# Operands of the products moved to multiples of 512 bytes from the weights, and the first block's 1/rms applied on VectorE alone

## Chip, cores and metric

The kernel runs on one core of one Trainium2 chip. The metric is device time in microseconds, the median of several executions. One more execution was profiled; its trace is what the rows below are read from.

## What is computed

Two blocks follow one another on a sequence of 2048 positions with 1024 features, in float32. The first norms x, multiplies it with w_in, and splits the result into a state space mixer (s5, with a gelu and a gated w_glu product) and a short convolution; both meet in w_out, a residual and a second norm. The second block has a modulation from w_ada, a convolution of seven taps, a two-way scan in chunks of 128 (ssd), a Fourier mix, an output product w_out2 and a gated feed-forward layer of width 2816.

```python
xn = rmsnorm(h, norm_gain[l])
proj = jnp.einsum('bld,dc->blc', xn, w_in[l])
...
v = gate_c * h                          # short_conv_mixer
y = sum(conv_w[k] * vp[:, k:k + seq] for k in range(CONV_K))
return gate_b * y
...
(jax.nn.silu(h @ w_gate) * (h @ w_up)) @ w_down      # swiglu
```

In the first block h, gate_c, gate_b and z_conv are all columns of proj, so each carries the factor 1/rms of its position.

## The kernel before

Features lie on the 128 partitions, positions along the free axis. The sequence is cut into four blocks of TB = 512 positions, and every large product works on one block: an output tile of 128 features by 512 positions is the sum over KD = 8 (or fewer) slices k of 128 input features.

Each float32 product is done as three products of a rounded type. `weights` (L100 to L112) loads a row of weights, wraw, of 4096 bytes per partition (issued by the SP queue, L106), rounds it into whi on ScalarE (L108) and takes the rest into wlo on VectorE (L111). The data is split the same way into a high and a low tile, such as xh and xl. `gemm` then issues 2 matmuls for each k with whi (L122 with the high, L123 with the low tile) and, after these, one for each k with wlo (L126). Every matmul has a weight load (PEld) of its own, of 128 columns or 512 bytes per partition; the moving operand is 512 columns or 2048 bytes. Slices of weights step by 512 bytes, slices of the data by 2048, so the distance between the two, modulo 512 bytes, is one and the same for all matmuls of a kind.

Which products have which data:

- xh, xl (L122, L123, L126): all of the first block's products and the second block's w_in2 and w_out2. The first norm's data for ctx has 256 columns.
- yh, yl: the four w_glu tiles of each block, four slices each.
- dxh, dxl: w_gate and w_up of the feed-forward layer, 44 tiles for each block of positions.
- hh, hl: w_down, in parts of three to five slices. The last part of the last block is done in two halves of 256 columns, with weights of its own in a pool e.
- uf (L1146 to L1148): here a slice of xh or xl is the stationary operand and 280 columns of a constant pair wfh, wfl move. A slice of those steps by 1120 bytes.

Where the tiles lie follows from the pools, which are stacked in the order in which they are opened: const, w, norm and hx (xh, xl) from the low end of a partition, others from the high end. After the feed-forward layer's start, hx is closed and the pool d with hh and hl begins where hx began. Every tile takes a multiple of 32 bytes. The norm pool holds 18 tiles of 16 bytes, which take 576 bytes, 64 more than 512; all else in w and norm is a multiple of 512. The addresses in a partition, in bytes, and their distance from the weights:

```
tile        first address            distance from whi and wlo, modulo 512
whi, wlo    32416 and 40608          -
xh, xl      67808 (and 3 more)       64
hh, hl      67808 (and 9 more)       64
dxh, dxl    176832, 193216           32
yh, yl      212960, 221152           320
```

In the last block's halves, hh and its weights in pool e are at distance 0. In uf the moving wfh is at distance 0 from xh at k = 0, and each k adds 1120 bytes; wfl is 256 further.

The order of the instructions of each engine is the program's, with priorities where `high_priority` raises them; each engine and each DMA queue works through its own list in order.

In block 0 the norm isn't applied to x ahead of the products: `first_prep` puts x times the gain into xh, xl, and 1/rms, as the tile r0 (128x512), is multiplied into the results. `h(j)` (L799) makes hs from a product: VectorE multiplies it by r0 (L803) and POOL by r0 again (L804), since hs meets a second unscaled product in `c(j)` (L815, cv). After the three taps POOL multiplies the sum cy by r0 (L825), and `g(j)` (L830) multiplies the next product into it. POOL also builds the s5 tables T at the time (L404 to L409, six products a step, from `s5_params`); a table is stored by a DMA of the SP queue (L620, Td). Next to these, `a1_prep` norms the next block's x: n_t on VectorE (L741), then xh on ScalarE and xl on VectorE (L137, L138).

`rstd` (L153) computes 1/rms from a sum of squares in some twelve tiny instructions on tiles of 128x4, in two buffers each; rs_b is one of them.

Of the kernel before, what the change touches and what calls it, by code (L numbers as in the profile page):

```python
# [10 lines left out]
F32R = mybir.dt.float32r  # L11
I32 = mybir.dt.int32
AF = mybir.ActivationFunctionType
ALU = mybir.AluOpType
# [3 lines left out]
P = 128  # L18
D = 1024
KD = 8  # L20
SEQ = 2048
TB = 512
# [39 lines left out]
class Kernel:  # L62
    def __init__(self, ctx, tc, A, stage=99):
        self.ctx, self.tc, self.A, self.nc = ctx, tc, A, tc.nc
        self.stage = stage
        self.uid = 0
        self.pool_lo = False
        self.ahead = 75


    def nm(self, s):
        self.uid += 1
        return f"{s}_{self.uid}"
# [79 lines left out]
    def rstd(self, acc, width, y=None):  # L153


        nc = self.nc
        c = acc.shape[1] // P
        ps = self.bank("nb", (P, c))
        for i in range(c):
            nc.tensor.matmul(ps[:, i:i + 1], lhsT=acc[:, i * P:(i + 1) * P],  # L160
                             rhs=self.ones[:, 0:1], start=True, stop=True)

        def tl(s, dt=F32):
            return self.t(self.np_, (P, c), f"rs_{s}", dt, bufs=2)

        v, h, y0, y1 = tl("v"), tl("h", I32), tl("y0"), tl("y1")
        y = self.t(self.np_, (P, c), "rs_y", bufs=6) if y is None else y
        nc.vector.tensor_scalar(v, ps, 1.0 / width, EPS, ALU.mult, ALU.add)
        nc.vector.tensor_single_scalar(h, v.bitcast(I32), 1, ALU.arith_shift_right)
        nc.vector.tensor_scalar(y0.bitcast(I32), h, -1.0, 1597463007.0, ALU.mult, ALU.add)  # L170
        a, b = tl("a"), tl("b")
        nc.vector.tensor_tensor(a, y0, y0, ALU.mult)
        nc.vector.tensor_tensor(a, a, v, ALU.mult)
        nc.vector.tensor_scalar(b, a, 0.375, -1.25, ALU.mult, ALU.add)
        nc.vector.tensor_tensor(b, b, a, ALU.mult)
        nc.vector.scalar_tensor_tensor(y1, b, 1.875, y0, ALU.add, ALU.mult)
        nc.vector.tensor_tensor(a, y1, y1, ALU.mult)
        nc.vector.tensor_tensor(a, a, v, ALU.mult)
        nc.vector.tensor_scalar(a, a, -0.5, 1.5, ALU.mult, ALU.add)
        nc.vector.tensor_tensor(y, y1, a, ALU.mult)  # L180
        return y
# [212 lines left out]
    def s5_params(self, pp):  # L394

        nc, A = self.nc, self.A
        st = {}

        def tl(s, sh=(P, NG), bufs=1):
            return self.t(pp, sh, s, bufs=bufs)  # L400
# [10 lines left out]
        def first():  # L411
# [74 lines left out]
            a, b = tl("pa", (P, NG, 8)), tl("pb", (P, NG, 8))  # L486
            for m in (1, 2, 4, 8):
                yield
                n = min(m, 15 - m)
# [14 lines left out]
            yield  # L504
            nc.vector.tensor_copy(self.E128[:, 0], Hr[:, :, 8])
            nc.vector.tensor_copy(self.E128[:, 1], Hi[:, :, 8])
            zero = tl("zero", (P, 1024))
            nc.vector.memset(zero, 0.0)
            for q in range(4):
                nc.sync.dma_start(out=self.Md[:, 8 * q:8 * q + 8, :],  # L510
                                  in_=zero.rearrange("p (g c) -> p g c", c=P))
            st["dsk"] = tl("dsk", (GH, NG))
            nc.sync.dma_start(out=st["dsk"], in_=A["s5_d"])
# [104 lines left out]
        def store(bt):  # L618

            nc.sync.dma_start(out=self.Td[bt], in_=st["T"])  # L620

        units = self.steps(first, 15)
        for bt in range(NG // G):
            units += self.steps(lambda bt=bt: matrices(bt), 3)
# [148 lines left out]
    def a1_units(self, b, ops):  # L773
        nc, A = self.nc, self.A
        st = {}
        tb, hf = divmod(b, 2)

        def mt(m):
            return self.mtile(A["w_in"][m], ops[b])

        def silu(out, ps):
            if b == 0:
                nc.vector.tensor_tensor(out, ps, self.r0, ALU.mult)
                ps = out
            nc.scalar.activation(out, ps, AF.Silu)

        def u(j):
            ps = mt(j)
            us = self.tmp("us")
            kt = lambda v: v.rearrange("p (k t) -> p k t", t=T8)  # L790
            uk = us.rearrange("p (t k) -> p k t", t=T8)
            if b == 0:
                nc.vector.tensor_tensor(uk, kt(ps), kt(self.r0), ALU.mult)
            else:
                nc.scalar.copy(uk, kt(ps))
            nc.sync.dma_start(out=self.Ud[tb, j * P:(j + 1) * P, :, hf * 64:(hf + 1) * 64],
                              in_=us.rearrange("p (t k) -> p t k", t=T8))

        def h(j):  # L799
            ps = mt(8 + j)  # L800
            st["hs"] = self.tmp("hs")
            if b == 0:
                nc.vector.tensor_tensor(st["hs"], ps, self.r0, ALU.mult)  # L803
                nc.gpsimd.tensor_tensor(st["hs"], st["hs"], self.r0, ALU.mult)  # L804
            else:
                nc.scalar.copy(st["hs"], ps)

        def c(j):
            ps = mt(16 + j)
            v = self.tmp("cv", (P, TB + 2))  # L810
            if b == 0:
                nc.vector.memset(v[:, 0:2], 0.0)
            else:
                nc.vector.tensor_copy(v[:, 0:2], self.ccarry[:, j])
            nc.vector.tensor_tensor(v[:, 2:], ps, st["hs"], ALU.mult)  # L815
            if b + 1 < NB:
                nc.vector.tensor_copy(self.ccarry[:, j], v[:, TB:TB + 2])
            y = self.tmp("cy")
            nc.vector.tensor_scalar(y, v[:, 2:], self.vec("conv_w", 8 + j), None, ALU.mult)
            nc.vector.scalar_tensor_tensor(y, v[:, 1:TB + 1], self.vec("conv_w", 4 + j), y,  # L820
                                           ALU.mult, ALU.add)
            nc.vector.scalar_tensor_tensor(y, v[:, 0:TB], self.vec("conv_w", j), y,
                                           ALU.mult, ALU.add)
            if b == 0:
                nc.gpsimd.tensor_tensor(y, y, self.r0, ALU.mult)  # L825
            st["y"] = y

        def g(j):
            ps = mt(12 + j)
            nc.vector.tensor_tensor(st["y"], ps, st["y"], ALU.mult)  # L830

        def z(j):
            ps = mt(20 + j)
            zs = self.tmp("zs")
            silu(zs, ps)
            nc.vector.tensor_tensor(zs, st["y"], zs, ALU.mult)
            nc.sync.dma_start(out=self.YCd[b, :, j], in_=zs)

        def zs(j):
            ps = mt(4 + j)  # L840
            t = self.tmp("zs")
            silu(t, ps)
            nc.sync.dma_start(out=self.ZSd[b, :, j], in_=t)

        units = [lambda j=j: u(j) for j in range(4)]
        for j in range(4):
            units += [lambda j=j, f=f: f(j) for f in (h, c, g, z)]
        units += [lambda j=j: zs(j) for j in range(4)]
        return units
# [860 lines left out]
    def run(self):  # L1710
# [3 lines left out]
        with ExitStack() as eh:  # L1714
            self.hp = self.pool("hx", 2, ctx=eh)
            left = self.run_ab(ops)
            if left is None:
                return
            self.ahead = 40
            g3, ((g1, prep1), (g2, prep2)) = left  # L1720
            self.tp = self.pool("tmpc", ctx=eh)
            with ExitStack() as es:
                u = self.ssd_units(3, self.pool("c", ctx=es))
                W(u[:4], g3[:3])
                W(u[4:10])
                W(u[10:13], g3[3:])
                W(u[13:28], prep2)
                W(u[28:], g2[:4])
            xp = self.pool("dx", side="right")

            def room():
                return tuple(self.t(xp, (P, KD, TB), n, F32R) for n in ("dxh", "dxl"))

            def dprep(b):
                return self.mod_prep(lambda k: self.X2d[b, :, k], lambda: self.rs[b],
                                     self.s2_x, self.sf_x, TB, ops, ("d", b), room)

            prep, prod, res = self.mix_units(3, self.hx, self.pool("o3", ctx=eh))
            W(prep, g2[4:])
            W(prod, prep1)  # L1740
            W(res + dprep(3), g1)
# [4 lines left out]
        for b in range(NB - 1, -1, -1):  # L1746
            main, cost, tail, res, ending = self.ffn_units(b, ops, dp)
            n = FQ[1]
# [20 lines left out]
    def run_ab(self, ops):  # L1769
# [4 lines left out]
        with ExitStack() as es:  # L1774
# [3 lines left out]
            with self.tc.high_priority(offset=30):  # L1778
                self.first_prep(ops)
            with ExitStack() as e2:  # L1780
                params = self.s5_params(self.pool("s5p", ctx=e2))
                n = len(params) // 2
                W(self.a1_units(0, ops), self.merge(params[:n], self.a1_prep(1, ops)))
                W(self.a1_units(1, ops), self.merge(params[n:], self.a1_prep(2, ops)))
# [19 lines left out]
        with ExitStack() as es:  # L1804
# [10 lines left out]
            n = (0, 9, 18, 27, 34)  # L1815
# [132 lines left out]
```

## Time and profile before

| | us |
|---|---|
| median of 3 runs (lowest, highest) | 3682.25 (3679.05, 3688.32) |
| the profiled execution | 3681.94 |
| its span, first to last instruction | 3680.1 |
| PE busy | 3507.8 |
| VectorE (DVE) busy | 2145.9 |
| ScalarE (ACT) busy | 1459.8 |
| GpSimd (POOL) busy | 988.2 |

The span leaves out 1.8 us of the execution's time. PE is TensorE's matmuls, PEld its weight loads, SPq the queue that issues most DMAs. The mean granted clock of TensorE is 0.98 of full speed. Matmul durations are modelled and overlap one another, so the pace of a run of matmuls is read from starts, not from durations.

### The profile page before, as it was taken

The numbers are of one execution on the slowest core, as the hardware profiler recorded it, in microseconds if no ns is written. First come the engines' busy times: TensorE is split into PE (matmuls) and PEld (weight loads), VectorE is DVE, ScalarE is ACT, GpSimd is POOL, SyncE is SP. The second block draws the span as 40 slices with busy tenths as digits, with TensorE's granted clock in tenths as the row PEclk, the third lists the DMA queues.
The fourth block names the chain that finished last, engine by engine and source line by source line (L and its number), as shares of the span: only waits on it lengthen the run. The fifth ranks groups of instructions, "written<-read, shape, count | busy, mean of one in ns | idle before, by whom it ended". The sixth has DMA issues, their size and how long they took to land. (4 is left out here: it accounts for less than half of the span.)

```text
span 3680.1 us, 46968 instructions
## 1 busy us (share of the span) xinstructions
PE 3507.8 (95%) x16602; PEld 2828.3 (77%) x16602; DVE 2145.9 (58%) x3986; ACT 1459.8 (40%) x2350; POOL 988.2 (27%) x938
## 2 busy tenths in 40 slices
PE   8799999898979999999999999999999999999998
PEld 6577888776778888776777788877888778887787
DVE  8764534456686677777666535665445664454334
ACT  3233232234444344335536533355333553333222
POOL 2864233232453353433223101131011210110001
PEclk9999999999989999999999999999999999999999
DMA  6457665677654565466554335443344433344232
GB/s 197 153 180 215 201 204 177 190 224 246 214 188 162 172 202 174 165 199 196 166 187 138 111 109 166 149 139 115 109 144 158 141 120 110 125 150 133 78 110 77
DMA packets 321932, 588.14 MB, mean 160 GB/s; under 512 B 73888, under 2 KB 150560, under 8 KB 320800
## 3 DMA queue, kind: packets, MB, share of 16 engines
q1 hardware_dynamic: 321696, 585.13, 50.2%
q8 instruction: 132, 2.16, 0.2%
q14 instruction: 104, 0.85, 0.1%
HBM read 472.63 MB, written 112.36 MB: 159 GB/s over the span
## 5 line engine op out<-in xcount | busy, mean ns | idle before, releaser
L108 ACT CAST whi<-wraw 128x1024 fp32r<-128x1024 f32 (+3 forms) x634 | 567.9, 897 | 1058.4 <-PE mm L123 772.1
L111 DVE TENSOR_TENSOR wlo<-wraw,whi 128x1024 fp32r<-128x1024 f32 (+3 forms) x516 | 539.8, 1047 | 725.5 <-PE mm L126 502.5
L122 PE MATMUL mm<-xh,whi 128*128 128x512 f32 (+1 forms) x2000 | 806.2, 405 | 64.9 <-ACT whi L108 42.5
L123 PE MATMUL mm<-xl,whi 128*128 128x512 f32 (+1 forms) x2000 | 790.7, 397 | 3.6 <-DVE xl L138 1.6
L148 POOL TENSOR_TENSOR n_acc<-n_acc,n_sq 128x512 f32<-128x512 f32 (+1 forms) x175 | 229.8, 1317 | 1371.7 <-ACT n_sq L147 1344.1
L123 PE MATMUL mm<-dxl,whi 128*128 128x512 f32 x1408 | 557.6, 396 | 0.8 <-DVE dxl L995 0.6
L122 PE MATMUL mm<-dxh,whi 128*128 128x512 f32 x1408 | 555.8, 395 | 1.9 <-ACT dxh L994 1.9
L122 PEld LDWEIGHTS mm<-xh,whi 128*128 128x128 f32 x2000 | 387.0, 194 | 156.7 <-ACT whi L108 53.4
L126 PE MATMUL mm<-xh,wlo 128*128 128x512 f32 (+1 forms) x2000 | 498.6, 391 | 4.8 <-DVE wlo L111 4.8
L123 PEld LDWEIGHTS mm<-xl,whi 128*128 128x128 f32 x2000 | 386.6, 193 | 86.2 <-DVE xl L138 4.4
L126 PEld LDWEIGHTS mm<-xh,wlo 128*128 128x128 f32 x2000 | 372.5, 190 | 86.5 <-DVE wlo L111 8.0
L111 POOL TENSOR_TENSOR wlo<-wraw,whi 128x1024 fp32r<-128x1024 f32 (+1 forms) x118 | 284.8, 2416 | 558.9 <-ACT whi L108 269.2
L126 PE MATMUL mm<-dxh,wlo 128*128 128x512 f32 x1408 | 360.5, 397 | 0.0
L123 PEld LDWEIGHTS mm<-dxl,whi 128*128 128x128 f32 x1408 | 264.0, 188 | 65.6 <-DVE dxl L995 2.0
L122 PEld LDWEIGHTS mm<-dxh,whi 128*128 128x128 f32 x1408 | 263.7, 187 | 64.4 <-ACT dxh L994 3.2
L126 PEld LDWEIGHTS mm<-dxh,wlo 128*128 128x128 f32 x1408 | 264.1, 188 | 63.8
L122 PE MATMUL mm<-hh,whi 128*128 128x512 f32 (+1 forms) x744 | 285.8, 391 | 2.5 <-ACT hh L137 2.3
L1035 DVE SCALAR_TENSOR_TENSOR cy<-mm,vecs,cy 128x504 f32<-128x504 f32 (+5 forms) x396 | 266.5, 689 | 30.4 <-ACT cy L1029 27.3
L123 PE MATMUL mm<-hl,whi 128*128 128x512 f32 (+1 forms) x744 | 280.7, 383 | 1.4 <-DVE hl L138 1.3
L126 PE MATMUL mm<-hh,wlo 128*128 128x512 f32 (+1 forms) x744 | 195.9, 380 | 0.0
L122 PEld LDWEIGHTS mm<-hh,whi 128*128 128x128 f32 x744 | 139.5, 188 | 33.0 <-ACT hh L137 5.6
L123 PEld LDWEIGHTS mm<-hl,whi 128*128 128x128 f32 x744 | 140.2, 188 | 30.2 <-DVE hl L138 5.0
(472 smaller groups left out, 4547.2 us busy)
## 6 DMA issues: line engine op xcount, KB each, us to landing
wraw<-w_in SPq DMA_DIRECT2D x186, 512.0 KB, 4.5
wraw<-w_gate SPq DMA_DIRECT2D x88, 512.0 KB, 3.6
wraw<-w_up SPq DMA_DIRECT2D x88, 512.0 KB, 3.5
wraw<-w_out SPq DMA_DIRECT2D x64, 512.0 KB, 3.8
mraw<-w_ada SPq DMA_DIRECT2D x96, 256.0 KB, 3.6
n_x<-xT SPq DMA_DIRECT2D x85, 256.0 KB, 4.7
n_x<-X1d SPq DMA_DIRECT2D x80, 256.0 KB, 4.1
n_x<-X2d SPq DMA_DIRECT2D x72, 256.0 KB, 3.8
```

The lines of the kernel that those rows point to most:

```text
L108: nc.scalar.copy(hi, raw)
L111: eng.tensor_tensor(lo, raw, hi.bitcast(F32), ALU.subtract)
L122: nc.tensor.matmul(ps, lhsT=hi[:, s], rhs=xh, start=k == ks[0], stop=False)
L123: nc.tensor.matmul(ps, lhsT=hi[:, s], rhs=xl, start=False, stop=False)
L126: nc.tensor.matmul(ps, lhsT=lo[:, s], rhs=rhs(k)[0], start=False, stop=k == ks[-1])
L148: nc.gpsimd.tensor_tensor(acc, acc, sq, ALU.add)
L1035: nc.vector.scalar_tensor_tensor(yr[:, :, lo:hi], pr[:, :, lo + d:hi + d], w(k), yr[:, :, lo:hi], ALU.mult, ALU.add)
```

## The change

Three edits move tiles. `rstd` takes its rs_b tiles (two buffers of 32 bytes) from the const pool, which lies ahead of the weights, and no longer from norm, which lies behind them: whi and wlo go up by 64 bytes, to 32480 and 40672, and hx and all behind it stay. A tile of 120 columns (480 bytes), written once by POOL, is allocated behind dxh and dxl, which move from 176832 to 176352. Between weights and xh, hh and dxh the distance is then a multiple of 512; yh and yl are at 256.

In block 0, hs is made by one VectorE multiplication with r02 = r0 x r0, a new tile that VectorE computes once, and VectorE does the multiplication of cy. To make room for r02, the tile of zeros that clears Md in DRAM is halved and stored eight times, not four.

```diff
+    def shift(self, pool, n):
+        self.nc.gpsimd.memset(self.t(pool, (P, n), "shift"), 0.0)
...
-        a, b = tl("a"), tl("b")
+        a, b = tl("a"), self.t(self.cp, (P, c), "rs_b", bufs=2)
...
-            zero = tl("zero", (P, 1024))
+            zero = tl("zero", (P, 512))
             nc.vector.memset(zero, 0.0)
-            for q in range(4):
-                nc.sync.dma_start(out=self.Md[:, 8 * q:8 * q + 8, :],
+            for q in range(8):
+                nc.sync.dma_start(out=self.Md[:, 4 * q:4 * q + 4, :],
                                   in_=zero.rearrange("p (g c) -> p g c", c=P))
...
             if b == 0:
-                nc.vector.tensor_tensor(st["hs"], ps, self.r0, ALU.mult)
-                nc.gpsimd.tensor_tensor(st["hs"], st["hs"], self.r0, ALU.mult)
+                nc.vector.tensor_tensor(st["hs"], ps, self.r02, ALU.mult)
...
             if b == 0:
-                nc.gpsimd.tensor_tensor(y, y, self.r0, ALU.mult)
+                nc.vector.tensor_tensor(y, y, self.r0, ALU.mult)
...
             def room():
-                return tuple(self.t(xp, (P, KD, TB), n, F32R) for n in ("dxh", "dxl"))
+                x = tuple(self.t(xp, (P, KD, TB), n, F32R) for n in ("dxh", "dxl"))
+                if not self.shifted:
+                    self.shifted = True
+                    self.shift(xp, 120)
+                return x
...
-                params = self.s5_params(self.pool("s5p", ctx=e2))
+                pp = self.pool("s5p", ctx=e2)
+                self.r02 = self.t(pp, (P, TB), "r02")
+                self.nc.vector.tensor_tensor(self.r02, self.r0, self.r0, ALU.mult)
+                params = self.s5_params(pp)
```

## Rows read from the trace of the kernel before

**Rows 1.** The page: head and part 1, busy time by engine (cut).

```profile
span 3680.1 us, 46968 instructions
PE 3507.8 (95%) x16602; PEld 2828.3 (77%) x16602; DVE 2145.9 (58%) x3986; ACT 1459.8 (40%) x2350; POOL 988.2 (27%) x938
```

**Rows 2.** Windows by stage: length; busy us (count) of PE, PEld, DVE, ACT, POOL; clock; DMA.

```profile
15.00:60.00 45.00, 41.86 (x186) 33.21 (x186) 43.62 (x189) 14.54 (x20) 13.58 (x9) 1.00 0.68 206
...
120.00:180.00 60.00, 43.58 (x175) 33.62 (x176) 46.62 (x75) 17.91 (x29) 49.56 (x78) 0.86 0.59 185
...
1866.00:3667.00 1801.00, 1778.16 (x8048) 1415.33 (x8048) 930.04 (x1567) 729.68 (x1211) 243.68 (x239) 1.00 0.41 127
```

**Rows 3.** PE's groups by line and form; count, busy us, mean ns, idle before.

```profile
L122 PE MATMUL mm<-xh,whi 128*128 128x512 f32 x1920 | 782.7, 409 | 59.3 <-ACT whi L108 42.5 <-ACT xh L758 7.5 <-ACT xh L137 6.4
...
L122 PE MATMUL mm<-dxh,whi 128*128 128x512 f32 x1408 | 555.8, 395 | 1.9 <-ACT dxh L994 1.9
...
L122 PE MATMUL mm<-hh,whi 128*128 128x512 f32 x664 | 266.0, 403 | 2.5 <-ACT hh L137 2.3
```

**Rows 4.** Windows of unbroken products, PE alone: length, busy (count), clock, DMA.

```profile
3578.75:3634.75 56.00, 56.00 (x242) 1.00 0.36 113
1793.49:1836.08 42.59, 42.59 (x187) 1.00 0.52 163
3266.67:3289.57 22.90, 22.90 (x101) 1.00 0.69 207
892.03:900.05 8.02, 8.02 (x36) 1.00 0.69 229
1061.34:1064.16 2.82, 2.82 (x26) 1.00 0.12 47
3636.57:3650.95 14.38, 14.38 (x121) 1.00 0.01 2
1379.35:1391.58 12.23, 12.23 (x97) 1.00 0.57 190
```

**Rows 5.** Timeline of PE, 112 to 129 us: start, length, what, idle before.

```profile
112.95 2.00 PE L126 MATMUL mm<-xh,wlo 128*128 128x512 f32 x8
...
125.77 0.80 PE L122 MATMUL mm<-xh,whi 128*128 128x512 f32 x1 [9.41 <-ACT whi L108]
126.36 0.63 PE L123 MATMUL mm<-xl,whi 128*128 128x512 f32 x1
...
128.92 0.63 PE L123 MATMUL mm<-xl,whi 128*128 128x512 f32 x1
```

**Rows 6.** Timeline of DVE, 105 to 133 us.

```profile
105.26 0.67 DVE L803 TENSOR_TENSOR hs<-mm,r 128x512 f32<-128x512 f32 x1
...
121.51 0.69 DVE L815 TENSOR_TENSOR cv<-mm,hs 128x512 f32<-128x512 f32 x1 [9.81 <-POOL hs L804]
...
131.97 0.69 DVE L830 TENSOR_TENSOR cy<-mm,cy 128x512 f32<-128x512 f32 x1 [3.29 <-POOL cy L825]
```

**Rows 7.** Timeline of POOL, 105 to 121 us.

```profile
105.74 2.26 POOL L407 TENSOR_TENSOR a<-Hr,Li 128x128 f32<-128x128 f32 x1
...
114.35 0.40 POOL L405 TENSOR_TENSOR a<-Hi,Li 128x128 f32<-128x128 f32 x1
...
120.22 1.26 POOL L804 TENSOR_TENSOR hs<-hs,r 128x512 f32<-128x512 f32 x1
```

**Rows 8.** Timeline of the SP queue, 119 to 121 us.

```profile
119.45 0.34 SPq L620 DMA_DIRECT2D Td<-T  x1
119.88 0.38 SPq L106 DMA_DIRECT2D wraw<-w_in  x1
```

**Rows 9.** Timeline of ACT at 123 us.

```profile
122.89 0.62 ACT L137 CAST xh<-n_t 128x512 fp32r<-128x512 f32 x1 [20.58 <-DVE n_t L741]
```

**Rows 10.** POOL's groups, first 200 us.

```profile
L804 POOL TENSOR_TENSOR hs<-hs,r 128x512 f32<-128x512 f32 x4 | 11.0, 2745 | 13.7 <-DVE hs L803 13.7
...
L825 POOL TENSOR_TENSOR cy<-cy,r 128x512 f32<-128x512 f32 x4 | 6.9, 1714 | 16.9 <-DVE cy L822 16.9
```

More of the change, by code (lines that the diff above doesn't have):

```diff
@@ L66, in __init__ @@
         self.uid = 0
-        self.pool_lo = False
+        self.pool_lo = self.shifted = False
         self.ahead = 75
+    def shift(self, pool, n):
+        self.nc.gpsimd.memset(self.t(pool, (P, n), "shift"), 0.0)
     def nm(self, s):
```

## The prediction

> **What bounds the kernel now.** I read the page's head first, then windows by stage, PE's groups, windows of PE alone inside unbroken products, and last the timelines of the first block. PE is busy for 95% of the span [rows 1]. In the feed-forward stretch, 1866 to 3667 us, it is busy for 1778 of 1801 us [rows 2]: nothing else can set the time there, and only a shorter matmul shortens it. One early stretch differs: from 120 to 180 us PE works 43.6 of 60 us and the mean granted clock is 0.86 [rows 2].
>
> So the question is what one matmul costs. The durations in PE's groups, 395 to 409 ns [rows 3], overlap one another and don't answer it. Inside a stretch without a break, the length divided by the starts in it does. A window's count holds, beside those, one or two instructions that began before it, so I divide by 240, 186, 100, 35, 24, 120 and 95 for the seven windows [rows 4]:
>
> - dxh and dxl, 512 columns: 56.00/240 = 233.3 ns
> - xh and xl: 42.59/186 = 229.0 ns
> - hh and hl: 22.90/100 = 229.0 ns
> - yh and yl: 8.02/35 = 229.1 ns
> - ctx, 256 columns: 2.82/24 = 117.5 ns
> - the last block's down products, 256 columns: 14.38/120 = 119.8 ns
> - uf, 280 columns: 12.23/95 = 128.7 ns
>
> All at full granted clock, so load of the DMA and the clock don't divide them: the slowest of the 512 column kinds has a DMA share of 0.36, the quick ones 0.52 to 0.69. What divides them in the same order is where the moving operand lies, modulo 512 bytes, from the weights: 32 for dxh, 64 for xh and hh, 320 for yh, 64 for ctx, 0 for the last block.
>
> How much is there to be had? At half the granted clock the same xh matmul has six starts in 128.92 - 126.36 = 2.56 us [rows 5], 426.7 ns, which is 512 columns at 1.2 GHz with nothing over. At 2.4 GHz the like would be 213.3 ns. So a full-speed matmul loses 15.7 ns at distance 64 and 20.0 ns at distance 32, and loses nothing at half speed. Something that is hidden at half speed collides at full speed, and it depends on the address. The weight load that runs beside each matmul is the one other stream of that kind.
>
> **The change part by part.** *dxh and dxl, distance 32 to 0.* The weights move up by the 64 bytes of two rs_b buffers, dxh down by 480, so the distance becomes 32 - 480 - 64 = -512. Three groups of 1408 [rows 3] are 4224 matmuls. No row has 512 columns at distance 0. Bounds: from below the 213.3 ns of [rows 5], a gain of 4224 x 20.0 = 84 us; from above the present 233.3, no gain. I take 229.0, because the two multiples of 64 that are on show, 64 and 320, give the same time [rows 4] and 0 is the next one: 4224 x 4.3 = 18.2 us gained. The stretch is PE's, so all of it shows.
>
> *xh, xl, hh, hl, distance 64 to 0.* Three groups of 1920 and of 664 [rows 3] are 7752 matmuls. Bounds: 213.3 ns, a gain of 122 us, and 233.3 ns as the worst distance on show, a loss of 33 us. I take no change, again because 64 and 320 agree. One pair of rows says otherwise: at 256 columns distance 0 costs 119.8 ns and distance 64 costs 117.5 ns [rows 4]. There the matmul is half as long while the weight load beside it is the same 128 columns, so I don't carry the 2.3 ns over, but it stands in the range. The 240 ctx matmuls go from 64 to 0: 0.6 us lost by that pair. yh and yl, 192 matmuls, end at distance 256, not 0: a multiple of 64 still, no change.
>
> The Trainium skill, "TensorE: Matmul & The Clock Gate", section "Step-by-step: what each phase is for", says that loading the next tile's weights takes no SBUF read bandwidth from the running matmul; the 229.0 against 233.3 ns of this trace does not agree with a loss of nothing. The same page's section "Back-to-back issue gap" gives N/2.4 + 2.5 ns for a warm matmul, 215.8 ns at 512 columns; as an estimate from that figure, alignment to it would be worth 176 us, about 3500 us in all.
>
> *The first block's factors on VectorE.* Removed from POOL: four hs products and four cy products, 17.9 us of POOL time [rows 10]. Added to DVE: four cy products and one r0 x r0, each like the 0.67 to 0.69 us of DVE's own 512-column products [rows 6], 3.4 us; the hs product on DVE stays, with another factor. What the removal frees is seen at 105 us. DVE wrote hs by 105.93, POOL came to it at 120.22 behind the s5 tables in its queue [rows 7], and DVE stood 9.81 us before cv [rows 6]. Behind cv on DVE are the n_t products, behind them ACT's xh, idle for 20.58 us [rows 9], behind that the cast of the next weights, and PE stands 9.41 us [rows 5]. The c product ends at 112.95 + 2.00 = 114.95, so cv could start 6.5 us sooner, and the next product too.
>
> Where does it go? The SP queue holds a table store, Td, until POOL has written the table, at 119.45, and the next weight load, wraw, is behind it at 119.88 [rows 8]. It stays late, and the product after next waits for it. POOL gets slower when DVE works: its 0.40 us product while DVE stood [rows 7] took 2.26 us at 105.74. So the lasting gain is POOL's saved time on this chain: two hs and two cy, 4 x 1.3 = 5 us by the 1.26 us that an undisturbed one takes, and some of the cold clock. I take 6 us. Bounds: 15 us if the waits of 9.81 and 3.29 us [rows 6] both go and nothing replaces them; 3 us lost if DVE's 3.4 us land in 15 to 60 us, where it is busy 43.62 of 45 us [rows 2].
>
> *The rest.* Eight stores of half a zero tile for four are four more issues on SP, some 0.4 us each by [rows 8], 1.5 us past which one weight load might be moved; the halved memset gives DVE back about as much as r0 x r0 takes. One POOL memset of 120 columns, when POOL is 14% busy [rows 2], is hidden. I count these as nothing, and 1.5 us if the cover is gone.
>
> **Sum.** The profiled execution took 3681.9 us, 1.8 us around its span, and is 0.3 us under the median of the runs shown, so the forecast serves both. 3681.9 - 18.2 - 6 + 0.6 = 3658 us.
>
> **The rivals.** *Clear run.* If the moving stream reads at twice the pace of the weight load, at distance 0 it starts with it and meets it again, 512 bytes on, just as the load ends: few collisions would be left. For it: the loss vanishes at half clock, so it is a matter of meeting. Against it: in uf the moving operand's distance goes through all eight multiples of 32 modulo 256 (the step is 1120 bytes a k), and the mean still has 128.7 - 116.7 = 12.0 ns over 280 columns at 2.4 GHz; one quick case in eight could hide there, but the last block at 0 is not quick. At 5 ns under 229.0: 7752 x 5 + 4224 x 9.3 = 78 us, with the 6 about 3598 us.
>
> *Aligned is worse.* The 256-column pair is right, and both streams asking for the same place at each start costs 2.3 ns more at 512 columns as well: 7752 x 2.3 - 4224 x 2.0 - 6 = +3, 3685 us, no change. If distance 0 costs what 32 does, 233.3 ns: +33 - 6, 3709 us, slower. It decides against the change from 2.9 ns upward: 11976 x 2.9 = 35 against 18.2 + 6 + 11.
>
> *Addresses do nothing.* The 4.3 ns go with dxh for another reason (its place at the far end of the partition, say), and the change doesn't do what it says. By the Trainium skill's rule on weight loads above, this is the case to expect. Only the first block is left: 3676 us, no measurable change. Against it: yh lies at the far end too and takes 229.1 ns [rows 4].
>
> **How the numbers follow.** A difference under 0.3%, 11 us, can't be told from no change here. Chances: dxh as quick as xh 0.43 (3658; its own range 3645 to 3671, the first block's bounds); clear run 0.24; addresses do nothing 0.12; aligned worse 0.21, half of it within 11 us of before and half beyond. Faster: 0.43 + 0.24, with a little of the third case, 0.68. Same: 0.20. Slower: 0.12. The range reaches to 3595, which takes in the clear run to 5 ns, and to 3690, which takes in aligned-worse to 3 us short of the point where it shows, 3693.
>
> **What would show it.** The same seven windows in the changed kernel: dxh at 229 ns is my forecast, 224 or less the clear run, 231 and more for xh the aligned-worse case, 233.3 and 229.0 unchanged the third. uf and the last block must stay at 128.7 and 119.8 ns, since neither distance changes. In the first block the 9.41 us gap before 125.77 should be mostly gone and a wait for wraw, behind Td, stand in its place; DVE should wait for POOL nowhere between L803 and L830. I am wrong in the main if xh moves by more than 2 ns either way, as 7752 matmuls carry each ns as 8 us.

## The result, and the profile after

The changed kernel takes 3640.92 us (median of 4 runs, 3638.66 to 3645.58), the kernel before beside it 3680.65 us (4 runs, 3676.82 to 3688.32): ratio 0.989, 95% interval 0.987 to 0.991. It is faster, by 40 us, where 24 were forecast. The profiled execution took 3638.66 us.

The head and the busy times of the changed kernel's page, then its windows by stage (columns as in [rows 2]):

```profile
span 3636.9 us, 46981 instructions
...
PE 3472.3 (95%) x16602; PEld 2831.2 (78%) x16602; DVE 2146.6 (59%) x3991; ACT 1461.8 (40%) x2350; POOL 968.9 (27%) x931
```

```profile
15.00:60.00 45.00, 41.81 (x189) 33.45 (x188) 43.59 (x191) 14.47 (x20) 12.09 (x8) 1.00 0.71 212
...
120.00:180.00 60.00, 42.85 (x170) 32.92 (x169) 40.53 (x71) 17.49 (x28) 51.24 (x81) 0.91 0.60 190
1866.00:3627.00 1761.00, 1734.92 (x7988) 1404.71 (x7988) 919.52 (x1555) 724.88 (x1204) 243.50 (x238) 1.00 0.41 128
```

The last of these is 40 us shorter than the 1801 us of [rows 2]; it holds 60 matmuls fewer, some 14 us at 229 ns each, and the rest is gain. PE is still what bounds it. Of the 43 us between the two profiled executions, the starts of PE's matmuls give 18 to what lies before the first dxh (1878.8 us before, 1860.7 after) and 25 to the feed-forward stretch behind it. The 18 are two single executions and rough: `e3_dx_alone` below issues the same matmuls as before up to its first dxh and gets there at 1866.3 us.

The windows that the prediction named, PE alone, in the order of [rows 4] (dxh, xh, hh, yh, ctx, the last block, uf); the steps in them, from one start to the next, are 240, 186, 100, 34, 22, 120 and 94:

```profile
2241.16:2295.56 54.40, 54.40 (x241) 1.00 0.69 225
1775.17:1817.36 42.19, 42.19 (x187) 1.00 0.50 164
2301.94:2324.63 22.69, 22.69 (x101) 1.00 0.65 206
875.89:883.65 7.76, 7.76 (x36) 1.00 0.69 231
1010.25:1012.89 2.64, 2.64 (x25) 1.00 0.58 217
3593.17:3607.56 14.39, 14.39 (x121) 1.00 0.01 2
1233.81:1245.92 12.11, 12.11 (x95) 1.00 0.45 142
```

| operand (distance before, after) | before, ns | forecast | after, ns |
|---|---|---|---|
| dxh (32, 0) | 233.3 | 229.0 | 226.7 |
| xh (64, 0) | 229.0 | 229.0 | 226.8 |
| hh (64, 0) | 229.0 | 229.0 | 226.9 |
| yh (320, 256) | 229.1 | 229.1 | 228.2, most steps 226 to 227 |
| ctx, 256 columns (64, 0) | 117.5 | 119.8 | 120.0 |
| last block, 256 columns (0, 0) | 119.8 | 119.8 | 119.9 |
| uf (all, all) | 128.7 | 128.7 | 128.8 |

The two that don't move stayed. The 512-column kinds came to one pace, one that no row of before shows (yh's window has some slower steps in it). In the trace before, the steps went 226, 229, 232 and again (xh), or 231, 235, 233, 234 (dxh); after, nearly every step in these windows is 226 or 227.

In the first block, PE's product that waited 9.41 us in [rows 5], and gaps of PE between 120 and 180 us (idle before, and what ended it):

```profile
115.35 1.05 PE L584 MATMUL ss<-C,X 128*16 128x128 f32 x8
116.33 0.50 PE L126 MATMUL mm<-xh,whi 128*128 128x512 f32 x1
...
123.25 0.50 PE L126 MATMUL mm<-xh,whi 128*128 128x512 f32 x1 [1.19 <-ACT whi L112]
...
131.10 3.67 PE L130 MATMUL mm<-xh,wlo 128*128 128x512 f32 x8 [3.93 <-DVE wlo L115]
...
164.56 0.50 PE L126 MATMUL mm<-xh,whi 128*128 128x512 f32 x1 [2.59 <-ACT whi L112]
...
178.23 0.79 PE L126 MATMUL mm<-xh,whi 128*128 128x512 f32 x1 [6.32 <-ACT whi L112]
```

The wait of 9.41 us of [rows 5] is gone: that product now starts at 116.33 for 125.77 us, without a gap. The product behind it waits 1.19 us, where it waited 1.72. No wait of DVE for POOL is left in the first 200 us. But the time is partly given back. The 16th weight cast whi (casts are counted from 0) comes 15.3 us sooner than before (109.4 for 124.7 us), the 20th 7.5 (148.1 for 155.6), the 24th 6.5 (183.2 for 189.8). Two views of the changed kernel show what took it. The SP queue:

```profile
117.08 0.34 SPq L624 DMA_DIRECT2D Td<-T  x1
117.51 0.38 SPq L110 DMA_DIRECT2D wraw<-w_in  x1
...
135.04 0.33 SPq L624 DMA_DIRECT2D Td<-T  x1
135.46 0.38 SPq L110 DMA_DIRECT2D wraw<-w_in  x1
```

ACT, 139 to 175 us:

```profile
139.99 1.04 ACT L112 CAST whi<-wraw 128x1024 fp32r<-128x1024 f32 x1 [3.99 <-DMA wraw<-w_in]
...
174.61 0.63 ACT L151 ACTIVATE n_sq<-n_x 128x512 f32<-128x512 f32 x1 [10.10 <-POOL n_acc L152]
```

The table store Td still holds the weight load wraw, as in [rows 8]. And the 6.32 us of PE at 178 us have another cause: the weight cast on ACT stands behind a square, n_sq, that waits for POOL's sum n_acc. The sum comes at 173.32 us, behind the tables in POOL's queue:

```profile
172.96 0.40 POOL L409 TENSOR_TENSOR a<-Hi,Li 128x128 f32<-128x128 f32 x1
173.32 3.95 POOL L152 TENSOR_TENSOR n_acc<-n_acc,n_sq 128x512 f32<-128x512 f32 x3
```

The same hold is in the trace before, where ACT waits three times for n_acc in the first 260 us, 11.2 us in all, the longest just ahead of a weight cast:

```profile
184.85 0.63 ACT L147 ACTIVATE n_sq<-n_x 128x512 f32<-128x512 f32 x1 [6.82 <-POOL n_acc L148]
```

### The profile page after: what moved, and what is told of

It reads as the page before. It is cut to its first block, busy times and chain, and to the rows that moved or that the text cites. A ratio compares the mean times of both kernels' runs of the same rounds, so it can differ in the third digit from the quotient of the medians.

```text
span 3636.9 us, 46981 instructions
## 1 busy us (share of the span) xinstructions
PE 3472.3 (95%) x16602; PEld 2831.2 (78%) x16602; DVE 2146.6 (59%) x3991; ACT 1461.8 (40%) x2350; POOL 968.9 (27%) x931
## 5 line engine op out<-in xcount | busy, mean ns | idle before, releaser
L127 PE MATMUL mm<-dxl,whi 128*128 128x512 f32 x1408 | 548.5, 390 | 1.4 <-DVE dxl L998 1.2
L130 PE MATMUL mm<-dxh,wlo 128*128 128x512 f32 x1408 | 350.3, 390 | 0.0
```

Of the source, the lines that this page charges most:

```text
L127: nc.tensor.matmul(ps, lhsT=hi[:, s], rhs=xl, start=False, stop=False)
L130: nc.tensor.matmul(ps, lhsT=lo[:, s], rhs=rhs(k)[0], start=False, stop=k == ks[-1])
```

## Experiments

Theory: a full-rate matmul's pace is set by the distance between its moving operand and its weights, and the first block's gain is separate. Rivals: the place alone of the operand decides, or the edits need one another. Line numbers are each kernel's own.

**Each part alone.** Four kernels cut the change in two ways. `e1_vector_alone` is before with VectorE's edits only:

```diff
-                nc.vector.tensor_tensor(st["hs"], ps, self.r0, ALU.mult)
-                nc.gpsimd.tensor_tensor(st["hs"], st["hs"], self.r0, ALU.mult)
+                nc.vector.tensor_tensor(st["hs"], ps, self.r02, ALU.mult)
...
-                nc.gpsimd.tensor_tensor(y, y, self.r0, ALU.mult)
+                nc.vector.tensor_tensor(y, y, self.r0, ALU.mult)
```

> The kernel before with the first block's edits alone (r02, cy on VectorE, the halved zeros); all tiles of products stay where they were. If places of operands make the gain: 512-column matmuls stay at 233.3 ns (dxh) and 229.0 ns (xh, hh), the first block ends about 6 us sooner, and the time is some 3674 us, a ratio of 0.998. If the first block's chain of waits is what mattered: 3650 us or less, ratio 0.992.

`e2_place_alone` is the changed kernel with these edits undone, which leaves the two that move operands, rs_b and the tile of 120 columns:

> The changed kernel without the first block's edits: rs_b in the const pool and the tile of 120 columns behind dxl, nothing else. If places make the gain: all 512-column matmuls at 226.7 ns as in the changed kernel, DVE still waits some 10 us for POOL's hs near 110 us, and the time is some 3646 us, ratio 0.991. If the first block mattered: 3670 us or more, ratio over 0.997.

`e3_dx_alone` is before with dxh and dxl moved to distance 0, xh and hh left at 64:

```diff
+                    self.shift(xp, 8)
```

> The kernel before with a tile of 8 columns (32 bytes) behind dxl and nothing else: dxh and dxl lie at distance 0, xh and hh stay at 64. If the pace of dxh passes into the time in full: 4224 x 6.6 ns = 28 us less, some 3651 us, ratio 0.9925. If waits in the feed-forward layer take a part of it, as the trace of the changed kernel hints: 18 to 22 us less, ratio 0.994 to 0.995.

`e4_xh_hh_alone` is before with xh and hh moved to 0, dxh kept at 32:

```diff
-        a, b = tl("a"), tl("b")
+        a, b = tl("a"), self.t(self.cp, (P, c), "rs_b", bufs=2)
...
+                    self.shift(xp, 112)
```

> The kernel before with rs_b in the const pool, and dxh moved so that it keeps distance 32: xh and hh at distance 0. If the pace passes in full: 7752 x 2.2 ns = 17 us less, 3662 us, ratio 0.9954. If the first block's stage and the hh products hide a part: 8 to 12 us less, ratio 0.997 to 0.998.

| kernel | ratio to before, 95% interval | in us of 3680 |
|---|---|---|
| dx alone (e3) | 0.9938 [0.9922, 0.9954] | -23 |
| xh and hh alone (e4) | 0.9983 [0.9970, 0.9997] | -6 |
| both places (e2) | 0.9914 [0.9897, 0.9932] | -32 |
| VectorE's edits alone (e1) | 0.9977 [0.9964, 0.9990] | -8 |
| all, a second time (e10, below) | 0.9905 [0.9889, 0.9920] | -35 |

The products fit: 0.9938 x 0.9983 = 0.9921 for e2's 0.9914, and 0.9914 x 0.9977 = 0.9891 for the 0.989 of the result. Within these intervals the parts add up, and none needs another. e1 and e2 came out as their first theory had it; e3's interval (17 to 29 us) holds both of its theories; e4's 6 us are under both of its theories, though its interval reaches into the second. Windows of e3, dxh (240 steps, 226.7 ns) and xh (185 steps):

```profile
2248.15:2302.55 54.40, 54.40 (x241) 1.00 0.69 225
1781.47:1824.63 43.16, 43.16 (x186) 1.00 0.50 160
```

and of e4, dxh (240 steps, 233.3 ns) and xh (185 steps, 226.7 ns):

```profile
2259.47:2315.47 56.00, 56.00 (x241) 1.00 0.67 219
1789.54:1831.48 41.94, 41.94 (x186) 1.00 0.51 165
```

Each pace follows its own operand, with one odd row: e3's xh, unmoved at 64, ran this stretch at 233.3 ns in place of 229.0, while most other stretches of the same kernel kept 229. Up to there e3 issues the same matmuls as before, at the same addresses, and before ran the like stretch at 229.0 [rows 4]. So distance 64 has two rhythms, and a long stretch can stay in the slower. What decides between them is open.

The 6 us of e4 (1 to 11 by the interval) are less than its pace promises: 7752 x 2.2 ns is 17 us. But 2.2 ns is the difference of settled stretches. Behind a break (a wait, or matmuls of another kind in between) steps are slower. Of the steps under 250 ns of xh, xl, hh and hl, the first nine behind a break take 229.9 ns on average in the trace before and 230.1 in e4's; the later ones take 228.9 and 226.7. The first nine gain nothing, and they are a third of the steps. Over all of these steps the difference is 229.2 - 227.9 = 1.3 ns, or 10 us for 7752, which the interval holds. Waits may have taken a part as well. The traces can't tell: e3, with the same matmuls as before up to its first dxh, gets there 12.4 us sooner, so single executions scatter by more than what is looked for.

**The distance itself.** `e5_sweep` is the changed kernel with the weights of w_gate and w_up beginning 0, 16, ... 496 bytes into a longer tile, so that one kernel runs dxh at 32 distances (one raw weight buffer less, to make room):

```diff
+            hi = self.t(pool or self.wp, (P, n + pad), "whi", F32R, bufs=bufs)[:, off:off + n]
...
+            pg = self.mtile(A["w_gate"][m], x, off=4 * ((2 * m + 5 * b) % 32))
```

> The changed kernel, but the weights of the feed-forward layer's w_gate and w_up products begin at 0, 16, 32 ... 496 bytes inside a tile that is 512 bytes longer, another value for each product; dxh and dxl don't move. (One buffer of raw weights fewer makes room, so waits between products may grow; the pace inside a product counts.) If the distance between moving operand and weights sets the pace: 226.7 ns at distance 0 and 256, about 229 at 64 and 320, 233 at 32, and the whole curve repeats after 256 bytes or fewer. If the place of dxh alone sets it: 226.7 ns for every product.

It ran once, as did the next three kernels, so only their pace is used. Windows of it, PE alone, the last 15 steps of a product each, at distances 0, 496, 480, 320, 256, 224, 160, 64 and 32:

```profile
2046.44:2049.84 3.40, 3.40 (x17) 1.00 0.22 58
2079.29:2082.69 3.40, 3.40 (x16) 1.00 0.84 265
2084.79:2088.29 3.50, 3.50 (x17) 1.00 0.49 150
...
2727.52:2730.95 3.43, 3.43 (x16) 1.00 0.90 309
2218.21:2221.61 3.40, 3.40 (x16) 1.00 0.48 154
...
2263.67:2267.17 3.50, 3.50 (x17) 1.00 0.68 228
1943.10:1946.62 3.52, 3.52 (x17) 1.00 0.53 154
...
2548.50:2551.93 3.43, 3.43 (x16) 1.00 0.85 238
2559.59:2563.09 3.50, 3.50 (x17) 1.00 0.48 150
```

3.40/15 = 226.7 ns, 3.43 is 228.7, 3.50 is 233.3, and 3.52 is 234.7, or 234.1 by the unrounded starts. dxh never moved, and its pace took every value of before. Means over the last 15 steps of all products of a distance, breaks left out (four to seven products each):

| distance | mean, ns | distance | mean, ns |
|---|---|---|---|
| 0 | 226.7 | 256 | 227.7 |
| 16 | 227.5 | 272 | 228.2 |
| 32 | 233.4 | 288 | 233.4 |
| 48 | 232.6 | 304 | 232.1 |
| 64 | 230.0 | 320 | 229.7 |
| 80 | 230.0 | 336 | 229.9 |
| 96 | 233.3 | 352 | 233.3 |
| 112 | 233.2 | 368 | 232.3 |
| 128 | 233.5 | 384 | 233.2 |
| 144 | 233.3 | 400 | 233.3 |
| 160 | 234.1 | 416 | 234.2 |
| 176 | 232.0 | 432 | 232.0 |
| 192 | 233.2 | 448 | 233.4 |
| 208 | 233.3 | 464 | 233.3 |
| 224 | 233.3 | 480 | 233.3 |
| 240 | 227.7 | 496 | 226.7 |

The two halves are one curve: it repeats every 256 bytes, with a narrow minimum at 0 and 16 bytes below it, and a half-good place at 64 and 80. The place of dxh alone is refuted: with dxh unmoved, the distance sets the pace of most products.

It doesn't set every one. One of six products at 368 ran at 226.7 ns where the others took 233.4, one of six at 240 at 233.6 where the others took 226.7, and one each at 64 and 320 at 233.3. The windows of the two at 368 (15 steps) and 240 (14 steps):

```profile
2152.18:2155.58 3.40, 3.40 (x17) 1.00 0.49 154
2947.08:2950.35 3.27, 3.27 (x16) 1.00 0.52 174
```

`e7_all_moved` is the opposite cut: weights, xh, hh and dxh all 96 bytes further on with no distance changed between them, yh alone brought to distance 160 (a small tile of the setup is reused to make room).

```diff
+        nc.vector.memset(const("pad", (P, 24)), 0.0)
...
-                    self.shift(xp, 120)
+                    self.shift(xp, 96)
```

> The changed kernel with everything 96 bytes further: weights, xh, hh and dxh, the distances as in the changed kernel (0), but yh and yl, which stay, at distance 160 and not 256. If the distance sets the pace: xh, hh and dxh stay at 226.7 ns, and yh goes from 226.7 to 234 ns, as the sweep has it for 160. If the places themselves matter: xh, hh, dxh leave 226.7 ns and yh stays.

Windows of it: yh (34 steps), dxh, ending with the start of the last one (239 steps):

```profile
880.51:888.47 7.96, 7.96 (x36) 1.00 0.71 236
2244.82:2299.00 54.18, 54.18 (x241) 1.00 0.70 226
```

dxh kept 226.7 ns with both operands at other places, so the place of the weights alone doesn't decide either; yh, which stayed, went to 7.96/34 = 234.1 ns, the value that the sweep has for 160.

**What the distance acts on.** `e6_half_load`: the dxl matmuls load and use only the first 64 columns of their weights.

```diff
+                nc.tensor.matmul(ps[0:64], lhsT=hi[:, s.start:s.start + 64], rhs=xl, start=False, stop=False)
```

> The changed kernel, but in the feed-forward layer's w_gate and w_up products the matmul with dxl uses only the first 64 columns of its weights; the other half of that partial product is left out. If the weight load beside a matmul costs it time: the dxh matmul, beside which a load of 64 columns runs, takes about 220 ns (half of the 13.3 ns over 213.3 gone), and the dxl matmul, beside which the full load runs, stays at 226.7. If the 13.3 ns are a fixed price of every matmul: 226.7 ns for both.

A miss for both. Window of it over seven pairs of dxh and dxl:

```profile
2115.62:2118.86 3.24, 3.24 (x15) 1.00 0.27 81
```

3.24/7 = 463 ns a pair, more than the 453.3 of two whole ones. Half the load doesn't halve the loss; it breaks the even rhythm, with steps of about 229 and 234 ns by turns. So the loss is not so much per loaded column. The edit also halves the rows of the output that this matmul writes, and what that does to the pace was not tried by itself.

`e8_reversed` is the sweep with dxh and dxl read from the last column to the first in the gate and up products:

```diff
+        self.gemm(ps, hi, lo, ks, lambda k: (x[0][:, k, ::-1], x[1][:, k, ::-1]) if rev else (x[0][:, k], x[1][:, k]))
```

> The sweep again, but in the w_gate and w_up products the moving dxh and dxl are read from their last column to their first (the output has the feed-forward layer's positions reversed in each block). If only where the two streams begin counts, the least pace of 226.7 ns is again found within 16 bytes of one distance and its repeat 256 bytes on. If the course of the two streams over the whole load counts, the curve changes: 229 ns or more at distances 0 and 256, and another order of the 32 distances.

Windows of it at distances 0, 496, 256 and 368, 15 steps each:

```profile
2044.39:2047.89 3.50, 3.50 (x17) 1.00 0.20 56
2577.84:2581.34 3.50, 3.50 (x17) 1.00 0.53 155
2217.03:2220.53 3.50, 3.50 (x17) 1.00 0.50 150
2150.50:2154.05 3.55, 3.55 (x16) 1.00 0.44 148
```

The minimum is gone: 233.3 ns at 0, 496 and 256, up to 236.7 at 368. The distance still counts, with the same period: most products at 80 and 112, and again at 336 and 368, take 236.4 to 236.7 ns, as do some at 16 and 272, and nearly all others 233.3. So the relative course of the two streams of addresses matters, and not only where they begin. That a backward read costs something by itself is not excluded.

**The first block.** The changed kernel ran again (`e10_after_again`) beside one with Td issued from POOL's queue (`e9_td_on_pool`):

```diff
-            nc.sync.dma_start(out=self.Td[bt], in_=st["T"])
+            nc.gpsimd.dma_start(out=self.Td[bt], in_=st["T"])
```

> The changed kernel as it is, on the same chip as the next run, so that the two can be compared: 3636 to 3646 us, ratio to before 0.989, both by its earlier runs.

> The changed kernel with the four table stores Td issued from POOL's own queue, in place of SP's, where three of them still stand ahead of a weight load (117.08, 135.04 and 155.12 us). If Td's hold on SP is what ended the first block's gain, the weight loads behind it start as soon as a buffer is free, PE's waits for the weight cast between 120 and 175 us (15.2 us in the first 260 us, the longest 6.3 us) go for the most part, and the 24th weight cast, now at 183.2 us, comes 5 to 10 us sooner: 3631 to 3636 us. Rival: the weights were late for other reasons (the casts on ACT and DVE, or n_x, for which DVE waits up to 8.7 us), or POOL loses its time to issuing; then the 24th cast stays within 2 us of 183.2, another wait stands in the place of the first, and the time stays at 3638 to 3644 us.

e10 took 3642.9 us, e9 3671.54: ratio 0.9986 [0.9972, 0.9999], 29 us slower than e10. Neither theory has that. The 20th cast came 12.6 us sooner than in the changed kernel, as expected of a free SP queue; the 24th came 36.3 us later. ACT of e9:

```profile
147.18 0.61 ACT L789 ACTIVATE zs<-zs 128x512 f32<-128x512 f32 x1
201.74 0.63 ACT L151 ACTIVATE n_sq<-n_x 128x512 f32<-128x512 f32 x1 [53.95 <-POOL n_acc L152]
```

its PE:

```profile
207.33 0.80 PE L126 MATMUL mm<-xh,whi 128*128 128x512 f32 x1 [56.57 <-ACT whi L112]
```

and its POOL:

```profile
192.72 0.19 POOL L619 COPY T<-Hi 128x4 f32<-128x4 f32 x1
...
200.45 1.26 POOL L152 TENSOR_TENSOR n_acc<-n_acc,n_sq 128x512 f32<-128x512 f32 x1
```

With the stores in its queue, POOL's order came out otherwise: n_acc, which the changed kernel has behind three tables and a part of the fourth, now stands behind five and a part of the sixth. ACT's squares wait for it, and the weight casts wait behind them. It is the hold that took 6.32 us of PE in the changed kernel, grown to 56.57 us. So the next two kernels put the 14 sums n_acc of blocks 1 and 2 on VectorE, with Td on POOL (`e11_td_pool_acc_dve`) and with Td on SP (`e12_acc_dve`):

```diff
-            nc.gpsimd.tensor_tensor(acc, acc, sq, ALU.add)
+            (nc.vector if self.sq_dve else nc.gpsimd).tensor_tensor(acc, acc, sq, ALU.add)
...
+                self.sq_dve = True
                 W(self.a1_units(0, ops), self.merge(params[:n], self.a1_prep(1, ops)))
                 W(self.a1_units(1, ops), self.merge(params[n:], self.a1_prep(2, ops)))
+                self.sq_dve = False
```

> The store Td on POOL's queue as in the run before, and the 14 sums n_acc of the squares of blocks 1 and 2 (7 each) on VectorE, so that they no longer stand behind POOL's tables. If the loss of that run was only the order on POOL (the second square on ACT waited 53.9 us for n_acc, behind five tables), the 20th weight cast comes at about 135 us as there, the 24th at 171 to 176 us in place of 219.6 and of 183.2, and the time is 3628 to 3636 us, under that of the changed kernel. Rival: DVE, with 14 more sums of some 0.7 us and the splits queued behind them, or the loads n_x, becomes what is late, and the 24th cast stays at 180 to 190 us: 3636 to 3646 us, no gain over the changed kernel.

> The changed kernel with the 14 sums n_acc on VectorE alone; Td stays on SP. In the changed kernel ACT waits 10.1 us for n_acc at 174.6 us, and PE 6.3 us for the cast behind it. If the table store on SP is the greater hold, the 20th cast stays at about 148 us and only the wait at 174 us goes: 24th cast at 177 to 181 us, 3635 to 3641 us. Rival: POOL, rid of the sums, brings its tables and so Td sooner, and this alone gives as much as both edits: 24th cast under 176 us; or DVE's 14 x 0.7 = 10 us come back on it, and the time stays at 3638 to 3646 us.

| kernel | 20th, 24th cast, us | median, us | ratio to before |
|---|---|---|---|
| changed (e10) | 148.8, 183.6 | 3642.9 | 0.9905 [0.9889, 0.9920] |
| Td on POOL (e9) | 135.4, 219.6 | 3671.5 | 0.9986 [0.9972, 0.9999] |
| sums on VectorE (e12) | 127.9, 172.9 | 3633.6 | 0.9877 [0.9856, 0.9899] |
| both (e11) | 127.5, 155.1 | 3612.3 | 0.9818 [0.9797, 0.9838] |

Windows of e11, 120 to 180 and 180 to 240 us:

```profile
120.00:180.00 60.00, 59.52 (x272) 48.44 (x271) 52.78 (x86) 23.89 (x36) 45.26 (x61) 1.00 0.72 223
180.00:240.00 60.00, 58.45 (x272) 47.67 (x271) 49.36 (x90) 19.37 (x27) 48.96 (x73) 1.00 0.66 200
```

PE is busy 59.5 of 60 us where it was busy 42.85, at a granted clock of 1.00 for 0.91. The gain of e11 is more than I had expected (24th cast 16 us sooner than the earliest time named, the run 16 us under the range). It beats both kernels; its interval and that of the changed kernel don't touch. e12 alone is 9 us under e10, and the intervals touch: its trace says a gain (24th cast 10.4 us sooner than in the changed kernel), its time leaves it open. Its first theory missed, as the 20th cast came at 127.9 and not at about 148 us; the rival's mark, a 24th cast under 176 us, came, but not "as much as both edits". What e12 still pays is Td on SP, this time ahead of the load n_x:

```profile
153.33 0.33 SPq L624 DMA_DIRECT2D Td<-T  x1
153.76 0.38 SPq L199 DMA_DIRECT2D n_x<-xT  x1
```

```profile
159.21 0.63 ACT L148 ACTIVATE n_acc<-n_x 128x512 f32<-128x512 f32 x1 [14.97 <-DMA n_x<-xT]
```

ACT stands 14.97 us for n_x, and PE 13.54 us for the weight cast behind it; in e11, with Td on POOL's queue, ACT waits 5.3 us for n_x at most, and PE 0.5 us for a weight cast in the first 240 us.

## Why the prediction came out as it did

- **What bounds the kernel: right.** PE's pace carried its gain into the time where PE was the only bound: dx alone 23 us measured (17 to 29 by the interval), 4224 x 6.6 = 28 by its settled pace, 26 by the steps of dx in the traces of before and e3 (968.4 and 942.4 us).
- **dxh and dxl: right in kind, short in size.** The term of 18.2 us failed at one choice: "because the two multiples of 64 that are on show, 64 and 320, give the same time [rows 4] and 0 is the next one". They agree because they are one place: the curve repeats after 256 bytes, and 320 is 64. The bounds, 213.3 and 233.3, held; the value is 226.7.
- **xh, xl, hh, hl: wrong.** The same inference gave "no change"; measured, 2.2 ns in settled stretches and 1.3 over all steps. By its own mark, "wrong in the main if xh moves by more than 2 ns", the step fell. The harm was small because e4 gave 6 us (1 to 11 by the interval).
- **ctx: right**, 120.0 ns at distance 0; and the refusal to carry the 256-column pair over to 512 columns was right too, though no row of before could show it. The two widths prefer different distances: 64 for 256 columns, 0 for 512.
- **yh: wrong by about 2 ns** in most steps, on 192 matmuls: under half a microsecond.
- **First block: right.** 6 us forecast; VectorE's edits alone gave 0.23%, 8 us (4 to 13). The gap of 9.41 us went as said, and Td in front of wraw took half of the gain back. Missed was a second hold, n_acc behind the tables. The trace before has it already (6.82 us at 184.85 us, above). e11, rid of both, is 25 us ahead of the changed kernel at the end of the last hh matmul of its trace (3597.1 for 3621.9 us).
- **The rest at nothing:** e1 contains the eight stores and the halved memset, and its gain of 8 us leaves no room for a sizeable loss.
- **The rivals.** *Aligned is worse* is true at 256 columns alone. *Addresses do nothing* fell with e3, e4 and e5. *Clear run* had its direction: the best distance is 0, and "224 or less" is not reached; 13.4 ns over 213.3 remain at every distance tried. That reading order matters (e8) suits a matter of meeting streams; half a load (e6) doesn't fit the simple count of meetings. The mechanism stays open; the curve is measured.

The Trainium skill, "TensorE: Matmul & The Clock Gate", "Step-by-step: what each phase is for", which has the weight load take no read bandwidth from the running matmul, is not the whole of it by e5: there the weights' address alone is worth 7.4 ns a matmul between distances 0 and 160. Whether read bandwidth is what the matmul loses, no run here shows.

Sum: 23.6 us forecast, 40 measured. By the runs, 23 for dx in place of 18.2, 6 for xh and hh in place of 0, 8 for the first block in place of 6: 37, and the rest is within the intervals. The 3640.9 us lie in the whole range, but below the main case's own 3645 to 3671; the range held because it reached down for the clear run, whose pace did not come. That part was luck.

## What to carry to other kernels

Where PE is the bound, divide the length of an unbroken stretch by its starts, count the steps behind a break apart, and set the pace beside the operands' distance: a regular pattern of unequal steps (226, 229, 232) was the mark of a distance that could be bettered, and a tile of some bytes is enough to move it. Two equal readings are no curve: before "no change" is taken from two points, ask whether they could be the same point of a period. When a wait is taken from an in-order queue, look at what is next in that queue and in the next engine's; here one queue's freedom cost 29 us until the other hold was gone, and the two together gave 31.

## What the runs showed of the hardware

- The pace of a 512-column matmul at full clock depends on the distance of the moving operand from the weights, with a period of 256 bytes: 226.7 ns at 0, 234.1 at 160 (e5, e7).
- The pace settles only after some nine steps without a break: at distance 0 the first nine take 230.1 ns on average, the later ones 226.7 (e4).
- 16 bytes below a multiple of 256 cost no more than the multiple itself (226.7 ns at 496, 227.7 at 240), 32 below cost 233.3.
- One distance can hold two rhythms: 64 ran at 229.0 and, in one stretch of e3, at 233.3 ns; in the sweep, single products at 64, 240, 320 and 368 left the pace of the others at their distance, the one at 368 for the better (226.7 for 233.4).
- Reading the moving operand backward takes the minimum away at every distance: 233.3 ns and up to 236.7.
- At 256 columns the order is turned: 117.5 ns at distance 64, 119.9 at 0.
